# Moving attention, key selection and gate work of a five-branch decoder trunk against each other

## The chip, the cores and the metric

The kernel runs on one core of a Trainium2 chip. The metric is the device time in microseconds (us) of one execution, as the median of several runs. A profiled execution gives the trace. PE is the matrix engine (TensorE), DVE the vector engine, ACT the scalar engine, POOL the GpSimd engine, and SP the engine whose queue issues the weight transfers.

## The reference

Two layers (DEPTH = 2) over 512 tokens of width 1024. Each layer normalises the residual stream, projects it once with `w_in` (1024 x 12388), and feeds five branches:

```python
xn = rms_norm(h, norm_g[l])
(a_q, a_k, a_v, i_q, i_k, i_w, b_cq, b_ckv, b_kr, c_q, c_k, c_v,
 d_u, d_v, e_q, gates, merge) = jnp.split(xn @ w_in[l], offsets, axis=-1)
branches = (dsa_branch(...),     # A: 8 heads, one shared key/value head, best 128 keys per query
            mla_branch(...),     # B: 8 heads from low-rank latents, causal
            diff_branch(...),    # C: 4 heads, each the difference of two softmaxes, causal
            sgu_branch(...),     # D: chunked causal gating
            memory_branch(...))  # E: 4 heads over 256 memory tokens
mixed = sum(sigmoid(merge[n]) * ((o * silu(gates[n])) @ w_branch[l, n]) for n, o in enumerate(branches))
h = h + mixed @ w_out[l]
```

In A an indexer scores all earlier keys for each query (4 small heads, relu, weighted sum). The best min(256, 512 // 4) = 128 keys of each query are kept, and the softmax runs over those. In C two 64-row score matrices are made per head; the second softmax is multiplied by a lambda and subtracted from the first. A final RMS norm closes the trunk. Everything is float32.

## The kernel before, in words

**Precision and dense work.** Every float32 operand is split into a high and a low part (ACT copies the high part, DVE subtracts it to get the low part), and every product is three matmuls: high x high, high x low, low x high. These are lines 453 to 455, the helper `three`. Weights arrive through SP's queue as 512 KB pieces (`raw`), are split on the fly into `wh` (ACT, line 368) and `wl` (DVE, line 371), and the order of the pieces is the order of the units below. Up to four pieces are in flight and one or two are split ahead.

**Attention chains.** A, B and C share one chain per step, where a step is one head and one block of 128 queries (four blocks per head, so 32 steps for A, 32 for B, 16 for C; a step of C has two score matrices). PE makes scores into PSUM (`pS`); DVE adds the mask and takes the row maximum (`softmax_head`, line 543) and scales it (`nm`, line 546); ACT takes the exponential with the row sum (line 548); DVE takes the reciprocal (553); ACT normalises (554); PE transposes (`pT`, line 563); ACT and DVE split the result (185, 186); PE multiplies with the values (`po`, 573 or, in C, 1135). In C the normalisation is lines 1124 to 1128 on DVE, and row norms with a power on POOL follow (244). The chain is software-pipelined in `attend`: scores of step k, normalisation of step k-1, transposes of step k-2.

**Key selection for A.** `indexer` makes the four indexer heads and keys, then for each of the query blocks 1, 2, 3 a score tile of 256, 384 or 512 columns, and then 16 rounds of the DVE instructions MAX8 (line 1005: the eight largest of a row) and MATCH_REPLACE8 (line 1006: strike them out). Block 0 needs no selection. A's softmax uses the result as its mask, and A's first step is the one of block 3.

**What sets the order.** The string `ORDER` is the list of dense units of a layer, written by hand. `gX0 gX1` are the gates of branch X, `mX0` to `mX3` its merge and branch projection; `qr q0 q1 k0 k1 v0 v1` are B's latent projections; `a` A's queries; `ws dv z du` D's parts; `f0 f1 fv` C's queries with keys, and values; `mem` the next layer's memory rows. `+x` starts a chain, `-x` forces all that is left of it, `!x` forces a small postponed job. A planner (`Pace`) lets each chain advance between dense matmuls: every dense triple of matmuls lets planner time go by (660 ns for three 512-column ones, `tick`), and each part of a chain yields the planner time after which its next part may come. In attention that is `PACE`, 900 ns per part, for all branches. By the code a gate unit takes 10.6 us of planner time, a merge unit 15.9 us, and a unit of 512 output columns (`a dv du fv f0 f1`) 21.1 us.

This order is the priority of a list scheduler that then places the instructions on the engines, takes an instruction early if an older one can't go yet, and allocates buffers. On the chip each engine runs its instructions in the order so fixed.

**Buffers.** Most working tiles are blocks of 128 x 512 float32 from one pool of `NB` = 35 (2 KB per partition each). Four tiles `p` hold softmax rows. Three PSUM banks (tag `a`) serve scores, transposes and small jobs; four (tag `m`) serve the dense units; one (`o`) the products with the values. POOL's queue issues the loads of the memory rows, of D's small weights and of the residual rows (`h`).

Of the kernel before, what the change touches and what calls it, by code (L numbers as in the profile page):

```python
# [8 lines left out]
F32 = mybir.dt.float32  # L9
# [18 lines left out]
C_DU, C_DV, C_EQ, C_GATE, C_MERGE = 3172, 3684, 4196, 4708, 7268  # L28


ORDER = ("-mem gE0 !ckvt !lat qr q0 !qr0 gE1 k0 v0 +mla0 mE0 q1 k1 mE1 -mla0 !qr1 v1 +mla1 mE2 mE3 a -mla1 +idx "
         "gB0 gB1 mB0 mB1 mB2 mB3 !aq +dsa ws fv dv f0 z du -dsa !df0 +df0 f1 -df0 !oD !df1 "
         "gD0 gD1 +df1 mD0 mD1 -df1 mD2 mD3 gA0 gA1 mA0 mA1 mA3 mA2 gC0 gC1 mem mC0 mC1 mC3 mC2")
NW = 5
NB = 35
NC4 = 6
NTR = 8
NP = 4
NRAW = 4
PACE = 900.0  # L40
LAG_ROPE = 5000.0
LAG_QROPE = 10125.0
LAG_RSTD = 4000.0
# [89 lines left out]
def trunk(tc, d, out, taps=None):  # L133
    nc = tc.nc
# [439 lines left out]
                         start=(kb == 0 and n == 0), stop=(kb == 3 and n == len(ts) - 1))  # L574


    def attend(steps, scores, norm, trans, pv, pv_rows=None):

        hist = []
        due, last_due = None, None  # L580
        n = len(steps)
        for k in range(n + 4):
            cur = None
            if k < n:
                cur = scores(*steps[k][:2])
            if 0 < k <= n:
                norm(hist[k - 1], *steps[k - 1][:2])
            if cur is not None:
                hist.append(cur())
            yield PACE  # L590
            if last_due is not None:
                pv(last_due)
                last_due = None
                yield PACE
            if due is not None:
                u, i, last = due
                due = None
                if pv_rows is not None:
                    pv_rows(u, i)
                    if last:  # L600
                        last_due = u
                        yield LAG_FLIP
                    yield PACE
                elif last:
                    pv(u)
                    yield PACE
            if 2 <= k < n + 2:
                u, i, last = due = steps[k - 2]
                trans(hist[k - 2], u, i)
                hist[k - 2] = None  # L610
                yield PACE
        if last_due is not None:
            yield LAG_FLIP
            pv(last_due)
# [31 lines left out]
    def layer(l, mm):  # L646
        w = d["w_in"][l]
        S = {}
# [37 lines left out]
        def mem_attention():  # L686
            sc = 128 ** -0.5

            def scores(h, j):
                ps = psa("pS")  # L690
                kh, kl = (z[h // 2][:, (h % 2) * 256:(h % 2) * 256 + 256] for z in (S["kTh"], S["kTl"]))
                for jj in range(2):
                    q = slice((2 * j + jj) * 128, (2 * j + jj) * 128 + 128)
                    three(ps[:, jj * 256:(jj + 1) * 256], S["eh"][h][:, q], S["el"][h][:, q], kh, kl, True, True)

                def rest():
                    p = pp.tile([128, 512], F32, tag="p", name="p")
                    m, nm, s = small(2, "m"), small(2, "nm"), small(2, "s")
                    V.tensor_reduce(out=m, in_=ps.rearrange("p (j c) -> p j c", j=2), axis=AX.X, op=ALU.max)
                    V.tensor_scalar(nm, m, -sc, None, op0=ALU.mult)  # L700
                    for jj in range(2):
                        c = slice(jj * 256, (jj + 1) * 256)
                        A.activation(p[:, c], ps[:, c], AF.Exp, bias=nm[:, jj:jj + 1], scale=sc,
                                     accum_out=s[:, jj:jj + 1])
                    return p, s
                return rest

            def norm(ps_, h, j):
                p, s = ps_
                r = small(2, "r")  # L710
                V.reciprocal(r, s)
                for jj in range(2):
                    c = slice(jj * 256, (jj + 1) * 256)
                    V.tensor_scalar(p[:, c], p[:, c], r[:, jj:jj + 1], None, op0=ALU.mult)

            def trans(ps_, h, j):
                p = ps_[0]
                ps = psa("pT")
                for kb in range(2):
                    for jj in range(2):  # L720
                        T.transpose(ps[:, kb * 256 + jj * 128:kb * 256 + jj * 128 + 128],
                                    p[:, jj * 256 + kb * 128:jj * 256 + kb * 128 + 128], ident)
                src = ps.rearrange("p (k c) -> p k c", k=2)
                dst = [z[:, :1024].rearrange("p (k c) -> p k c", k=2)[:, :, j * 256:(j + 1) * 256] for z in pf]
                split(dst[0], dst[1], src)

            def pv(h):
                o = pso()
                c = slice(h * 128, h * 128 + 128)
                for kb in range(2):  # L730
                    three(o, S["mvh"][kb][:, c], S["mvl"][kb][:, c], pf[0][:, kb * 512:(kb + 1) * 512],
                          pf[1][:, kb * 512:(kb + 1) * 512], kb == 0, kb == 1)
                oT["E"][h] = blk(F32, "oE")
                A.activation(oT["E"][h], o, AF.Copy)

            yield 1500.0
            yield from attend([(h, j, j == 1) for h in range(4) for j in range(2)], scores, norm, trans, pv)
            tap(f"oE{l}", oT["E"][0])

        def go_mem():  # L740
# [189 lines left out]
        def mla_attention(hf):  # L930
            sc = 96 ** -0.5

            def scores(h, i):
                L = 128 * (i + 1)
                N = max(256, L)
                rows = slice(0, 96) if h % 2 == 0 else slice(0, 128)
                q = slice(i * 128, i * 128 + 128)
                ps = psa("pS")
                three(ps[:, :N], S["qh"][h][rows, q], S["ql"][h][rows, q], S["kh"][h][rows, :N],
                      S["kl"][h][rows, :N], True, True)  # L940
                return lambda: softmax_head(ps, L, cm[:, 512 - 128 * i:640], sc)

            def pv(h):
                o = pso()
                v = lambda kb: S["V"][kb][h // 4][:, h % 4, :, :].rearrange("p z c -> p (z c)")
                pv_causal(o, lambda kb: [(v(kb), 0), (v(kb), 1)])
                if h % 2 == 0:
                    oT["B"][h // 2] = blk(F32, "oB")
                r = slice(64 * (h % 2), 64 * (h % 2) + 64)
                add_halves(oT["B"][h // 2][r], o)  # L950

            yield 1500.0
            yield from attend(causal_steps(range(4 * hf, 4 * hf + 4)), scores,
                              lambda ps_, h, i: normalise(*ps_, 128 * (i + 1)),
                              lambda ps_, h, i: transposes(ps_[0], i), pv)
            if hf == 1:
                tap(f"oB{l}", oT["B"][0])
# [15 lines left out]
        def indexer():  # L973
# [10 lines left out]
            S["mb"] = [None] * 4  # L984
            for i in (1, 2, 3):
                L = 128 * (i + 1)
                sc = blk(F32, "score")
                S["mb"][i] = sc
                for hh in range(4):
                    ps = psa("pI")  # L990
                    q = S["iqs"][hh][:, i * 128:(i + 1) * 128]
# [5 lines left out]
                                           in1=cm[:, 512 - 128 * i:640] if hh == 0 else sc[:, :L],  # L997
                                           op0=ALU.mult, op1=ALU.add)
                    yield 900.0
                if i == 3:  # L1000
                    S["iqs"] = S["ki"] = None
                tap(f"score{l}_{i}", sc[:, :L])
                for _ in range(16):
                    m8 = small(8, "m8")
                    V.max(out=m8, in_=sc[:, :L])
                    V.match_replace(out=sc[:, :L], in_to_replace=m8, in_values=sc[:, :L], imm_value=GONE)
                    yield 700.0 + 2.0 * L
                V.tensor_scalar(sc[:, :L], sc[:, :L], -2e38, NEG, op0=ALU.is_gt, op1=ALU.mult)

        S["qs"] = [None] * 8  # L1010
# [28 lines left out]
        def dsa_attention():  # L1039
# [13 lines left out]
            def pv(h):  # L1053
# [3 lines left out]
                if h % 2 == 0:  # L1057
# [2 lines left out]
                add_halves(oT["A"][h // 2][r], o)  # L1060

            yield 500.0
            yield from attend(causal_steps(range(8)), scores,
                              lambda ps_, h, i: normalise(*ps_, 128 * (i + 1)),
                              lambda ps_, h, i: transposes(ps_[0], i), pv)
            tap(f"oA{l}", oT["A"][0])
# [36 lines left out]
        def diff_attention(hf):  # L1103
# [3 lines left out]
            def scores(e, i):  # L1107
                L = 128 * (i + 1)
                N = max(256, L)
                q = slice(i * 128, i * 128 + 128)  # L1110
                pss = []
                for s in range(2):
                    r = slice(64 * s, 64 * s + 64)
                    ps = psa("pS")
                    three(ps[:, :N], X["q"][e][0][r, q], X["q"][e][1][r, q], X["k"][e][0][r, :N],
                          X["k"][e][1][r, :N], True, True)
                    pss.append(ps)
                return lambda: [softmax_head(ps, L, cm[:, 512 - 128 * i:640], sc) for ps in pss]

            def norm(ps_, e, i):  # L1120
# [26 lines left out]
            def flip(e):  # L1147
                p = psa("pN")
                for i in range(4):
# [3 lines left out]

            X["o"] = {}
            yield 2500.0
            yield from attend(causal_steps(range(2)), scores, norm,
                              lambda ps_, e, i: transposes(ps_[0][0], i), flip, pv_rows)


# [339 lines left out]
```

## Time and profile before

| | |
|---|---|
| median of 3 runs | 1887.15 us (1886.16 to 1887.18) |
| profiled execution | 1887.75 us, of which its span is 1885.7 us |
| PE busy | 1802.5 us, 96% of the span |
| DVE busy | 1187.3 us, 63% |
| ACT busy | 947.3 us, 50% |
| POOL busy | 66.1 us, 4% |
| mean granted PE clock | 0.981 |

The span runs from the first to the last recorded instruction; 2.05 us of the profiled execution lie around it. Matmuls overlap in the pipeline, so the busy time of PE is a union and its idle time is what no matmul covers; the duration of one matmul is longer than the distance between two starts. The granted clock is listed beside each stretch of time: below 1.00 the array ran part of that stretch at a lower clock. The two layers are alike: what stands at time t of the first layer recurs some 932 us later.

### The profile page before, as it was taken

To read this page: it belongs to the slowest core of one execution; us is meant where nothing else is said; L and a number is where in the kernel's file an instruction comes from. 1 tells how busy PE (TensorE), PEld (TensorE's weight loads), DVE (VectorE), ACT (ScalarE), POOL (GpSimd) and SP (SyncE) were. 2 spreads that over 40 slices of the span, in tenths; PEclk is the share of its full clock that TensorE was granted. 3 is DMA by queue.
4 is the path that set the end of the run, shared out by engine and by line. 5 is a ranking of instruction groups with operands and counts; after the bars stand their busy time and mean duration, and the time that the engine had idled before them with its cause. 6 is when DMAs were issued, how large, how long until landed. Compare 5 with 4: busy or idle time off the path is not lost.

```text
span 1885.7 us, 24863 instructions
## 1 busy us (share of the span) xinstructions
PE 1802.5 (96%) x8793; PEld 1489.3 (79%) x8793; DVE 1187.3 (63%) x3009; ACT 947.3 (50%) x2127; POOL 66.1 (4%) x133
## 2 busy tenths in 40 slices
PE   7999999998899999999999999999898999999998
PEld 6878888886777778888887888888776776788887
DVE  7548756996656664445465577579967467544544
ACT  7457765426554553234355567653275545432333
POOL 1000000000000010000000000010000000000000
PEclk9999999999989999999999999999998999999999
DMA  6223222331212223333352332133311111233331
GB/s 230 73 73 87 62 79 84 95 90 45 68 34 57 68 73 106 101 116 97 117 174 56 73 98 68 56 101 101 90 44 47 56 56 57 74 94 101 118 127 69
DMA packets 151589, 161.02 MB, mean 85 GB/s; under 512 B 26293, under 2 KB 130793, under 8 KB 151465
## 3 DMA queue, kind: packets, MB, share of 16 engines
q1 hardware_dynamic: 148520, 149.21, 26.9%
q0 software_dynamic: 2944, 10.23, 1.6%
q8 instruction: 69, 1.13, 0.3%
q14 instruction: 56, 0.45, 0.1%
HBM read 155.22 MB, written 4.19 MB: 85 GB/s over the span
## 4 chain that ended last, share of the span: by engine, by line
PE 87%; DVE 7%; ACT 5%; issue 1%; DMA 0%; POOL 0%; POOLq 0%; SPq 0%; DVEq 0%; ACTq 0%
PE pm L453 25%; PE pm L454 25%; PE pm L455 25%; PE po L573 2%; PE pT L563 1%; PE pS L453 1%; DVE ptl L186 1%; DVE wl L371 1%; ACT p L548 1%; PE pS L454 1%; PE pS L455 1%; PE po L1135 1%; ACT p L554 1%; ACT pth L185 1%; PE pa L1020 1%
## 5 line engine op out<-in xcount | busy, mean ns | idle before, releaser
L371 DVE TENSOR_TENSOR wl<-raw,wh 128x512 fp32r<-128x512 f32 x556 | 376.2, 682 | 362.2 <-ACT wh L368 350.9
L368 ACT ACTIVATE wh<-raw 128x512 fp32r<-128x512 f32 x556 | 346.0, 625 | 512.5 <-PE pm L454 334.1
L453 PE MATMUL pm<-xh,wh 128*128 128x512 f32 x1040 | 410.3, 395 | 4.4 <-ACT nat L1013 1.7
L454 PE MATMUL pm<-xl,wh 128*128 128x512 f32 x1040 | 408.8, 393 | 0.0
L455 PE MATMUL pm<-xh,wl 128*128 128x512 f32 x1040 | 408.0, 393 | 0.0
L453 PEld LDWEIGHTS pm<-xh,wh 128*128 128x128 f32 x1040 | 196.4, 189 | 46.3 <-ACT nat L1013 2.2
L455 PEld LDWEIGHTS pm<-xh,wl 128*128 128x128 f32 x1040 | 196.2, 189 | 41.1 <-issue 0.7
L454 PEld LDWEIGHTS pm<-xl,wh 128*128 128x128 f32 x1040 | 196.4, 189 | 39.6 <-issue 0.6
L453 PE MATMUL pm<-wh,xh 128*128 128x512 f32 x512 | 202.1, 399 | 1.2 <-DVE acc L1304 1.2
L455 PE MATMUL pm<-wh,xl 128*128 128x512 f32 x512 | 202.5, 397 | 0.0
L454 PE MATMUL pm<-wl,xh 128*128 128x512 f32 x512 | 201.1, 393 | 0.0
L548 ACT ACTIVATE p<-p,nm 128x512 f32<-128x512 f32 (+1 forms) x192 | 107.3, 559 | 71.3 <-DVE nm L546 68.2
L453 PE MATMUL pm<-yh,wh 128*128 128x512 f32 x320 | 125.8, 393 | 0.0
L454 PE MATMUL pm<-yl,wh 128*128 128x512 f32 x320 | 125.6, 392 | 0.0
L455 PE MATMUL pm<-yh,wl 128*128 128x512 f32 x320 | 125.2, 391 | 0.0
L453 PEld LDWEIGHTS pm<-wh,xh 128*128 128x128 f32 x512 | 96.1, 188 | 22.3 <-issue 2.0
L455 PEld LDWEIGHTS pm<-wh,xl 128*128 128x128 f32 x512 | 96.2, 188 | 20.7 <-issue 0.5
L454 PEld LDWEIGHTS pm<-wl,xh 128*128 128x128 f32 x512 | 96.3, 188 | 18.2
L563 PE MATMUL pT<-ident,p 128*128 128x128 f32 x400 | 76.7, 294 | 34.2 <-ACT p L554 28.3
L186 DVE TENSOR_TENSOR ptl<-pT,pth 128x512 fp32r<-128x512 f32 (+3 forms) x176 | 88.6, 504 | 32.5 <-ACT pth L185 32.0
L185 ACT ACTIVATE pth<-pT 128x512 fp32r<-128x512 f32 (+3 forms) x176 | 78.7, 449 | 56.5 <-PE pT L563 40.9
L543 DVE CUSTOM_DVE_ANT_0 p<-pS,cm 128x128 f32<-128x128 f32 (+3 forms) x144 | 66.5, 462 | 47.0 <-PE pS L455 36.8
(337 smaller groups left out, 2940.1 us busy)
## 6 DMA issues: line engine op xcount, KB each, us to landing
raw<-w_in SPq DMA_DIRECT2D x176, 512.0 KB, 3.6
raw<-w_branch SPq DMA_DIRECT2D x40, 512.0 KB, 3.5
raw<-w_in SPq DMA_DIRECT2D x36, 256.0 KB, 3.0
raw<-mem_w_kv SPq DMA_DIRECT2D x16, 512.0 KB, 5.2
raw<-w_out SPq DMA_DIRECT2D x16, 512.0 KB, 3.8
raw<-mla_w_uq SPq DMA_DIRECT2D x18, 128.0 KB, 3.4
xrow<-x SPq DMA_DIRECT2D x4, 512.0 KB, 7.4
raw<-mla_w_ukv SPq DMA_DIRECT2D x16, 128.0 KB, 2.5
```

The source lines that it names most:

```text
L185: A.activation(hi, src, AF.Copy)
L186: V.tensor_tensor(out=lo, in0=src, in1=f32(hi), op=ALU.subtract)
L368: A.activation(hv, raw, AF.Copy)
L371: V.tensor_tensor(out=lv, in0=raw, in1=f32(hv), op=ALU.subtract)
L453: T.matmul(o, ah, bh, start=st, stop=False)
L454: T.matmul(o, ah, bl, start=False, stop=False)
L455: T.matmul(o, al, bh, start=False, stop=sp)
L543: V.tensor_tensor_reduce(out=p[:, :L], in0=ps[:, :L], in1=mask, op0=ALU.add, op1=ALU.max, scale=1.0, scalar=GONE, accum_out=m)
L548: A.activation(p[:, :L], p[:, :L], AF.Exp, bias=nm, scale=scale, accum_out=s)
L554: A.activation(p[:, :L], p[:, :L], AF.Copy, scale=r)
L563: T.transpose(ps[:, kb * 128:(kb + 1) * 128], p[:, kb * 128:(kb + 1) * 128], ident)
L573: T.matmul(o[:, q0:], v, pf[part][:, kb * 384 + q0:kb * 384 + 512], start=(kb == 0 and n == 0), stop=(kb == 3 and n == len(ts) - 1))
```

## The change

Six things are changed.

1. **Early selection.** `+idx` moves from behind `-mla1` to right behind `!lat`, ahead of B's projections. All three score tiles are now made first, which lets the indexer's query and key tiles go; then the 48 rounds follow, each pair of instructions yielding 1500 + 3.0 L instead of 700 + 2.0 L ns of planner time (L = 256, 384, 512).
2. **Longer steps.** `attend` takes the branch's name, and `PACE` is 900 ns for E, 1200 for B, 1900 for A, 1600 for C.
3. **The order.** `mE2` and `gB0` now lie inside B's two halves. A's attention starts ahead of `mB0` to `mB3` and runs beside them too. `fv` goes behind `du`. C's first half is no longer forced right behind `f1`: it runs beside `f1 gD0 gD1 mD0 mD1`, and its second half beside `mD2 mD3 gA0 gA1 mA0 mA1`.
4. **Paired scores in C.** The two 64-row score matrices of a step are written alternately, product by product, into two PSUM banks, instead of one after the other. The products are the same.
5. **41 blocks** instead of 35.
6. The scratch memory for the descriptors of POOL's transfers is set to 4096 bytes, which makes room for the blocks.

```diff
-ORDER = ("-mem gE0 !ckvt !lat qr q0 !qr0 gE1 k0 v0 +mla0 mE0 q1 k1 mE1 -mla0 !qr1 v1 +mla1 mE2 mE3 a -mla1 +idx "
-         "gB0 gB1 mB0 mB1 mB2 mB3 !aq +dsa ws fv dv f0 z du -dsa !df0 +df0 f1 -df0 !oD !df1 "
-         "gD0 gD1 +df1 mD0 mD1 -df1 mD2 mD3 gA0 gA1 mA0 mA1 mA3 mA2 gC0 gC1 mem mC0 mC1 mC3 mC2")
+ORDER = ("-mem gE0 !ckvt !lat +idx qr q0 !qr0 gE1 k0 v0 +mla0 mE0 q1 k1 mE1 mE2 -mla0 !qr1 v1 +mla1 mE3 a gB0 -mla1 gB1 "
+         "!aq +dsa mB0 mB1 mB2 mB3 ws dv f0 z du fv -dsa !df0 +df0 f1 !oD gD0 gD1 mD0 mD1 -df0 !df1 "
+         "+df1 mD2 mD3 gA0 gA1 mA0 mA1 -df1 mA3 mA2 gC0 gC1 mem mC0 mC1 mC3 mC2")
-NB = 35
+NB = 41
-PACE = 900.0
+PACE = {"E": 900.0, "B": 1200.0, "A": 1900.0, "C": 1600.0}
...
-    def attend(steps, scores, norm, trans, pv, pv_rows=None):
+    def attend(branch, steps, scores, norm, trans, pv, pv_rows=None):
+        gap = PACE[branch]
...
-            yield PACE
+            yield gap
...
             for i in (1, 2, 3):
                 L = 128 * (i + 1)
-                sc = blk(F32, "score")
-                S["mb"][i] = sc
+                sc = S["mb"][i] = blk(F32, "score")
...
-                if i == 3:
-                    S["iqs"] = S["ki"] = None
+            S["iqs"] = S["ki"] = None
+            for i in (1, 2, 3):
+                L = 128 * (i + 1)
+                sc = S["mb"][i]
                 for _ in range(16):
                     m8 = small(8, "m8")
                     V.max(out=m8, in_=sc[:, :L])
                     V.match_replace(out=sc[:, :L], in_to_replace=m8, in_values=sc[:, :L], imm_value=GONE)
-                    yield 700.0 + 2.0 * L
+                    yield 1500.0 + 3.0 * L
...
-                pss = []
-                for s in range(2):
-                    r = slice(64 * s, 64 * s + 64)
-                    ps = psa("pS")
-                    three(ps[:, :N], X["q"][e][0][r, q], X["q"][e][1][r, q], X["k"][e][0][r, :N],
-                          X["k"][e][1][r, :N], True, True)
-                    pss.append(ps)
+                pss = [psa("pS") for _ in range(2)]
+                rows = [slice(64 * s, 64 * s + 64) for s in range(2)]
+                for n, (a, b) in enumerate(((0, 0), (0, 1), (1, 0))):
+                    for ps, r in zip(pss, rows):
+                        T.matmul(ps[:, :N], X["q"][e][a][r, q], X["k"][e][b][r, :N], start=n == 0, stop=n == 2)
...
-    nc = bacc.Bacc("TRN2", target_bir_lowering=False, num_devices=1)
+    nc = bacc.Bacc("TRN2", target_bir_lowering=False, num_devices=1, dynamic_dma_scratch_size=4096)
```

More of the change, by code (lines that the diff above doesn't have):

```diff
@@ L593, in attend @@
                 last_due = None
-                yield PACE
+                yield gap
             if due is not None:
@@ L602, in attend @@
                         yield LAG_FLIP
-                    yield PACE
+                    yield gap
                 elif last:
                     pv(u)
-                    yield PACE
+                    yield gap
             if 2 <= k < n + 2:
@@ L610, in attend @@
                 hist[k - 2] = None
-                yield PACE
+                yield gap
         if last_due is not None:
@@ L736, in mem_attention @@
             yield 1500.0
-            yield from attend([(h, j, j == 1) for h in range(4) for j in range(2)], scores, norm, trans, pv)
+            yield from attend("E", [(h, j, j == 1) for h in range(4) for j in range(2)], scores, norm, trans, pv)
             tap(f"oE{l}", oT["E"][0])
@@ L952, in mla_attention @@
             yield 1500.0
-            yield from attend(causal_steps(range(4 * hf, 4 * hf + 4)), scores,
+            yield from attend("B", causal_steps(range(4 * hf, 4 * hf + 4)), scores,
                               lambda ps_, h, i: normalise(*ps_, 128 * (i + 1)),
@@ L1062, in dsa_attention @@
             yield 500.0
-            yield from attend(causal_steps(range(8)), scores,
+            yield from attend("A", causal_steps(range(8)), scores,
                               lambda ps_, h, i: normalise(*ps_, 128 * (i + 1)),
@@ L1155, in diff_attention @@
             yield 2500.0
-            yield from attend(causal_steps(range(2)), scores, norm,
+            yield from attend("C", causal_steps(range(2)), scores, norm,
                               lambda ps_, e, i: transposes(ps_[0][0], i), flip, pv_rows)
```

## The prediction

> **What bounds the kernel now.** The page's slices and its chain come first.
>
> ```profile
> PE   7999999998899999999999999999898999999998
> DVE  7548756996656664445465577579967467544544
> ```
> ```profile
> PE 87%; DVE 7%; ACT 5%; issue 1%; DMA 0%; POOL 0%; POOLq 0%; SPq 0%; DVEq 0%; ACTq 0%
> ```
>
> PE holds the end, and its low slices lie in the attention of each layer. So only two things can shorten the run: PE's idle or slow-clocked time, and PE's own work. The next view cuts the run by stage; its columns are engine busy times with instruction counts, the granted PE clock and DMA.
>
> ```profile
> core 0: us, PE busy (x) PEld busy (x) DVE busy (x) ACT busy (x) POOL busy (x), PEclk, DMA share, GB/s
> 147.00:172.00 25.00, 25.00 (x141) 21.74 (x140) 22.86 (x45) 17.25 (x32) 0.00 (x0) 1.00 0.34 90
> 172.00:302.00 130.00, 125.34 (x641) 105.15 (x640) 81.82 (x238) 89.06 (x204) 0.00 (x0) 1.00 0.21 64
> 302.00:347.00 45.00, 45.00 (x223) 37.73 (x222) 35.58 (x73) 25.96 (x48) 5.64 (x6) 1.00 0.41 118
> 347.00:410.00 63.00, 63.00 (x280) 52.24 (x279) 61.61 (x148) 20.86 (x36) 0.00 (x0) 1.00 0.34 100
> 410.00:548.00 138.00, 119.40 (x558) 95.92 (x557) 95.21 (x290) 82.72 (x204) 2.68 (x4) 0.90 0.16 46
> 565.00:708.00 143.00, 136.69 (x649) 105.53 (x648) 91.37 (x313) 70.09 (x190) 11.82 (x20) 0.96 0.22 67
> 708.00:855.00 147.00, 147.00 (x650) 121.71 (x649) 68.22 (x105) 49.31 (x84) 1.08 (x2) 1.00 0.36 108
> 1342.00:1480.00 138.00, 118.69 (x557) 95.52 (x555) 94.10 (x289) 81.82 (x203) 2.67 (x4) 0.90 0.16 46
> 1497.00:1638.00 141.00, 133.56 (x643) 101.95 (x642) 91.07 (x313) 69.48 (x188) 9.66 (x16) 0.99 0.21 61
> ```
>
> In the first layer B's attention is 172 to 302, selection 302 to 434, A's attention 410 to 548 and C's 565 to 708; the last two rows are A and C of the second layer. The dense stretch 708 to 855 has no idle time and gives the price of a 512-column matmul, 147.00 / 650 = 0.226 us, and of DVE beside gates and merges, 68.22 / 147 = 0.46 us per us. A loses 138 - 119.40 = 18.6 us of idle and, at clock 0.90, up to 0.10 x 138 = 13.8 us of speed. B has as many steps of nearly the same chain and loses 130 - 125.34 = 4.7 us at full clock. C loses 6.3 us idle and 0.04 x 143 = 5.7 us of clock, in the second layer 7.4 and 1.4. What ends A's waits, and the worst of them:
>
> ```profile
> PE pT L563 <- ACT p L554: 12.6, 5, 6.1
> ```
> ```profile
> 429.56 0.39 PE L455 MATMUL pm<-wh,xl 128*128 128x512 f32 x1
> 436.00 0.69 PE L563 MATMUL pT<-ident,p 128*128 128x128 f32 x2 [6.05 <-ACT p L554]
> ```
> ```profile
> 432.80 0.43 DVE L1008 TENSOR_SCALAR score<-score 128x512 f32<-128x512 f32 x1
> 433.26 0.69 DVE L543 CUSTOM_DVE_ANT_0 p<-pS,score 128x512 f32<-128x512 f32 x1
> ```
>
> Of the stretch's waits, 12.6 us end with the normalised row that the transposes need. In the worst one selection ends on DVE at 433.2, A's first softmax starts at once, and PE stands at the transposes although dense matmuls follow in its order: the chain is too near behind its own inputs.
>
> **A's attention, longer steps.** By the code A yields 76 times: 68 us of planner time at 900 ns, 144 at 1900. Ahead of its forced end lie four units and `z`, 87 us; with `mB0` to `mB3` it is 151. (A triple counts 0.66 us in the planner and 3 x 0.226 = 0.68 on PE.) Now the chain has about 4.3 us of dense work per step instead of 2.0, more than B has today. No instruction of A is added. If A then loses what B loses, 4.7 us, the gain per layer is between 18.6 - 4.7 = 13.9 (idle alone) and 18.6 + 13.8 - 4.7 = 27.7 us; the second layer has 14.6 to 28.4. I take **26 a layer, -52**, near the upper end, because PE was mostly busy while slow: its rows give 119.40 us busy at a mean clock of 0.90. The bounds for two layers are 0 (the waits only move) and -66 (all of it). [...]
>
> **C's attention, no forced end.** A half of C yields 30 times and waits twice for a flip, 31 us with its lead, beside `f1`, 21 us; the rest is forced out without dense work. At 1600 it is 52 us beside 74, and 84 for the second half. Of 12.0 and 8.8 us lost I leave 4 each: 8.0 + 4.8, **-13**; bounds 0 and -21.
>
> **C's paired scores.** The trace already holds pairs: the scheduler put two score products of different row halves side by side wherever both banks were free.
>
> ```profile
> 581.46 0.39 PE L454 MATMUL pm<-wl,xh 128*128 128x512 f32 x1
> 581.77 0.38 PE L453 MATMUL pS<-kh,qh 64*128 64x256 f32 x1
> ...
> 582.32 0.50 PE L455 MATMUL pm<-wh,xl 128*128 128x512 f32 x1
> 582.66 0.40 PE L453 MATMUL pm<-wh,xh 128*128 128x512 f32 x1
> ```
> ```profile
> 592.67 0.28 PE L1135 MATMUL po<-dv,ptl 128*128 128x256 f32 x1
> 592.88 0.51 PE L453 MATMUL pS<-kh,qh 64*128 64x512 f32 x2
> ...
> 593.78 0.50 PE L453 MATMUL pm<-wh,xh 128*128 128x512 f32 x1
> 594.12 0.40 PE L454 MATMUL pm<-wl,xh 128*128 128x512 f32 x1
> ```
> ```profile
> 1589.86 0.39 PE L455 MATMUL pm<-yh,wl 128*128 128x512 f32 x1
> 1590.18 0.39 PE L453 MATMUL pS<-kh,qh 64*128 64x256 f32 x2
> ...
> 1590.73 0.39 PE L1135 MATMUL po<-dv,pth 128*128 128x256 f32 x1
> 1590.96 0.28 PE L1135 MATMUL po<-dv,ptl 128*128 128x256 f32 x1
> ```
>
> One unpaired half of 256 columns costs 582.66 - 581.46 less two dense matmuls, 1.20 - 0.45 = 0.75 us. Both halves paired cost 1590.96 - 1589.86 less one dense matmul and one 256-column product (half a dense one, 0.11), 0.76 us: the second half is free. At 512 columns both halves cost 594.12 - 592.67 - 0.11 - 0.226 = 1.11 us. So a new pair saves 0.75 to 1.11 us. Of the 32 score steps 8 are paired already (the first at 592.88, the last at 1590.18) and 4 partly: 20 new pairs save 15 us, with the parts and the wide ones up to 19. I take **-13**; bounds 0 and -19. [...] I expect most pairs to form because at 1600 ns the banks are read before the next step.
>
> **Early selection beside B.**
>
> ```profile
> L1005 DVE MAX8 m<-score 128x8 f32<-128x256 f32 (+2 forms) x96 | 53.2, 558 | 1.4
> L1006 DVE MATCH_REPLACE8 score<-m,score 128x256 f32<-128x256 f32 (+2 forms) x96 | 52.2, 544 | 0.1
> ```
> ```profile
> 410.00:434.00 24.00, 17.97 (x38) 1.00 0.30 87
> ```
>
> The rounds take (53.2 + 52.2) / 2 = 53 us of DVE per layer. Until now they ran beside dense units, and DVE was full (61.61 of 63 us) while PE lost nothing; they ended late all the same, at 433, and held A (the last row is the score tile's DVE time behind 410). From the start of B's projections to A, DVE does 22.9 + 81.8 + 35.6 + 61.6 + 18.0 = 220 us. `mB0` to `mB3` leave this stretch: 65 us of PE, and at 0.46 some 30 of DVE. What is left is 190 us of DVE in 263 - 65 = 198 of PE, 96%, and B's chain, today at 81.8 / 130 = 63%, runs in it. Queued behind a round on DVE are B's maxima, reciprocals and low parts, for which ACT and PE wait, and the `wl` parts. No row shows this mix. From below: B's 4.7 us a layer vanish, as its steps grow from 900 to 1200 ns, -9. From above: B stalls as A does, +27.7 a layer, +55. I take **+12**, nearer to the lower end, because a full DVE cost PE nothing in 347 to 410, and the rounds, at 1500 + 3 L, leave gaps. The planner gives selection 141 us in 139, so one round is forced at A's start; if it is late again, A waits, but `mB0` to `mB3` now lie behind A's first scores as dense work.
>
> **At nothing.** Moved gates and merges keep their instructions, and PE had no gap beside them. Their weights follow them in SP's queue, four pieces ahead. More blocks only allow earlier allocation. For POOL's scratch:
>
> ```profile
> h<-hscr POOLq DMA_DIRECT2D x4, 512.0 KB, 4.7
> ```
> ```profile
> 1831.47 1.05 POOL L1382 DMA_DIRECT2D h<-hscr  x2 [83.16 <-PE pm L455]
> ```
> ```profile
> 1851.84 0.69 DVE L1393 SCALAR_TENSOR_TENSOR h<-pm,h 128x512 f32<-128x512 f32 x1
> ```
>
> Even if its transfers had to go one behind the other, four such loads would take 19 us, and 20 us lie between the issue of the last ones and their first use. Without that cover they cost up to 10 us over both layers; there is no reason for a gain.
>
> **Sum.** -52 - 13 - 13 + 12 = -66 us. The profiled execution took 1887.75 us (span 1885.7 and 2.05 around it), which gives 1821.75; the median of the runs is 0.6 lower, so **1821 us**.
>
> **Rivals.** (1) *Selection spoils B*: half of the upper bound, +27.7 instead of +12, with PE standing at B's transposes: 1837; at the full bound 1864. For it: 96% of DVE. Against: DVE at 98% without loss in 347 to 410. (2) *A's waits move*: the chain is bound by its own latency, or starts late, and A saves only the lower bound, 28 instead of 52: 1845. For it: ACT and DVE are busy only 60 and 69% in A and PE waits all the same. Against: B's rows. (3) *Slower: DVE becomes the bound from B's projections to A.* With chains beside it DVE reaches only the share it has in A, 95.2 / 138 = 69%; then 190 us of DVE take 275 instead of 198 us, +77 a layer against a gain of 39 (26 + 6.5 + 6.5): 1887 + 2 x 38 = 1963. It decides below a DVE share of 190 / (198 + 39) = 80%. [...] Against: 302 to 347 ran at 79% without idle PE. (4) *It does nothing*: one loss replaces the other, 1887.
>
> **Chances and range.** Forecast 0.66 (own range 1800 to 1838), (1) 0.14, (2) 0.12, (3) 0.05, (4) 0.03. The low end, 1793, is -66 - 21 of the bounds for A and C with 13 for pairs and +5 for B. The high end, 1865, holds (2) and (1) at its full bound. A difference under 0.2% can't be told from none. Faster 0.92, same 0.03, slower 0.05.
>
> **What would show it.** Right: A's stretch at clock 1.00 with under 8 us idle; no single wait above 3 us; rows of `pS` in C with x2 in most steps; PE near 98% busy. Wrong: PE waits of B's `pT` or `pS` on DVE adding up to more than 10 us a layer; selection ending far behind A's first scores with PE idle; waits on ACT's row as before.

## The result and the profile after

| | before | changed |
|---|---|---|
| median | 1887.16 us (1886.16 to 1887.64, 4 runs) | 1830.05 us (1825.94 to 1834.69, 4 runs) |
| profiled execution (its span) | 1887.75 us (1885.7) | 1825.94 us (1823.9) |
| mean granted PE clock | 0.981 | 0.996 |

The ratio is 0.9699, with a 95% interval from 0.9669 to 0.9729: 57 us less, where 66 were forecast. The four runs of the changed kernel fall on two levels, 1826 (twice) and 1834 (twice), which widens the interval; the last section comes back to this. The profile is of a run on the lower level, so sums from the profiles come to 62 us instead of 57.

From the page of the changed kernel, busy time by engine, PE's slices and the chain's shares:

```profile
PE 1774.7 (97%) x8793; PEld 1470.2 (81%) x8793; DVE 1179.6 (65%) x3009; ACT 944.0 (52%) x2127; POOL 67.7 (4%) x133
...
PE   7999999999999999999999999999999999999998
...
PEclk9999999999999999999999999999999999999999
...
PE 93%; DVE 4%; ACT 1%; issue 1%; DMA 0%; SPq 0%; POOL 0%; POOLq 0%; DVEq 0%; ACTq 0%
```

The low slices of A and C are gone, and PE's share of the chain that ended last rose from 87 to 93%. The same stages as windows of the changed kernel (columns as in the prediction's table). In the first layer 107 to 351 is the lead-up, from the end of E's attention to A's first scores, with the selection and B in it; 351 to 539 is A, 547 to 696 is C. The last three rows are the same three stages of the second layer.

```profile
107.00:351.00 244.00, 231.05 (x1163) 191.78 (x1161) 197.17 (x525) 148.10 (x321) 8.41 (x16) 1.00 0.28 79
147.00:351.00 204.00, 191.05 (x967) 158.09 (x965) 177.86 (x479) 128.79 (x275) 5.20 (x6) 1.00 0.27 77
351.00:539.00 188.00, 186.63 (x918) 155.78 (x919) 117.24 (x312) 108.99 (x248) 2.96 (x4) 0.99 0.25 73
547.00:696.00 149.00, 149.00 (x710) 116.15 (x707) 98.50 (x310) 69.00 (x182) 7.43 (x12) 1.00 0.25 75
1008.00:1252.00 244.00, 232.98 (x1164) 193.10 (x1162) 198.58 (x524) 148.46 (x321) 8.44 (x16) 0.99 0.28 79
1252.00:1441.00 189.00, 187.18 (x921) 156.16 (x922) 117.74 (x313) 109.50 (x248) 2.97 (x4) 0.99 0.25 73
1448.00:1628.00 180.00, 180.00 (x862) 142.04 (x862) 117.35 (x355) 84.93 (x219) 10.50 (x16) 1.00 0.26 77
```

The lead-up of the kernel before, in the same view:

```profile
107.00:408.00 301.00, 296.34 (x1464) 248.78 (x1463) 218.78 (x543) 172.04 (x363) 8.84 (x16) 1.00 0.30 84
```

A is idle for 1.4 us where it lost 18.6, C for nothing. The lead-up got worse: 13.0 us idle against 4.7, though it holds fewer units. PE's waits over the whole of the changed kernel say the same. The columns are who waited for whom, the total in us, how often, and the longest:

```profile
PE pa L225 <- DMA vec<-mla_kv_norm_g: 6.7, 1, 6.7
PE pm L453 <- DVE acc L1304: 5.0, 4, 1.9
PE pm L453 <- DVE sg L1278: 4.4, 4, 1.5
PE po L453 <- ACT pth L185: 3.5, 4, 1.5
PE pI L992 <- DVE iqs L965: 3.3, 2, 1.6
```

The largest entry of the kernel before, the wait of the transposes for ACT's normalised row, has gone from the list:

```profile
PE pT L563 <- ACT p L554: 28.3, 12, 6.1
```

What has come are single waits under 2 us: for gates (`sg`) and for the indexer's queries (`iqs`), which the list before does not have, and for merges (`acc`), 5.0 us instead of 2.5. The wait at the top of the list is in both kernels (6.8 us before).

**One yardstick for all kernels.** For each matmul I take the distance from its start to the next start in the trace, less the usual distance of its width in the traces of both kernels (227 ns for 512 columns, 174 for 384, 119 for 256, 109 for 128). The usual distances add up to 1727.4 us in both kernels, so the whole difference lies in what is left over, called *lost time* below. It holds waits, slow clock and the cost of the 64-row scores together.

| lost time, us (layer 1 / layer 2) | before | changed |
|---|---|---|
| lead-up (indexer, selection, B) | 8.5 / 8.5 | 19.4 / 19.6 |
| A's attention | 34.4 / 34.5 | 5.6 / 5.5 |
| C's attention | 21.6 / 20.8 | 8.1 / 8.3 |
| all else, both layers | 16 | 16 |

A gave 58 us, C gave 26, the lead-up took 22 back. The sum is 62, and the two profiled executions differ by 1887.75 - 1825.94 = 61.8.

### The profile page after: what moved, and what is told of

It reads as the page before. It is cut to its first block, busy times and chain, and to the rows that moved or that the text cites. A ratio compares the mean times of both kernels' runs of the same rounds, so it can differ in the third digit from the quotient of the medians.

```text
span 1823.9 us, 24819 instructions
## 1 busy us (share of the span) xinstructions
PE 1774.7 (97%) x8793; PEld 1470.2 (81%) x8793; DVE 1179.6 (65%) x3009; ACT 944.0 (52%) x2127; POOL 67.7 (4%) x133
## 4 chain that ended last, share of the span: by engine, by line
PE 93%; DVE 4%; ACT 1%; issue 1%; DMA 0%; SPq 0%; POOL 0%; POOLq 0%; DVEq 0%; ACTq 0%
PE pm L453 27%; PE pm L454 26%; PE pm L455 26%; PE po L573 2%; PE pT L563 2%; PE pS L1117 2%; PE po L1135 1%; DVE wl L371 1%; PE pa L526 1%; PE pS L455 1%; PE pS L454 1%; PE pS L453 1%; DVE score L1008 1%; PE pS L1050 1%; PE pa L1022 1%
## 5 line engine op out<-in xcount | busy, mean ns | idle before, releaser
L453 PEld LDWEIGHTS pm<-wh,xh 128*128 128x128 f32 x512 | 96.1, 188 | 20.2 <-issue 2.2
L554 ACT ACTIVATE p<-p,r 128x512 f32<-128x512 f32 (+3 forms) x128 | 71.6, 559 | 24.7 <-DVE r L553 24.4
```

Source lines behind the costliest of these rows:

```text
L453: T.matmul(o, ah, bh, start=st, stop=False)
L554: A.activation(p[:, :L], p[:, :L], AF.Copy, scale=r)
```

## The experiments

Theory L says that the longer steps carry A's gain. Theory D says that the rounds of the selection, now on DVE beside B, cost the lead-up its new loss. Theory P1 says that pairs of scores do not form because two banks are not free together. The rivals stand with each run. All changes are made to the changed kernel unless "before" is named.

### Is it the rounds? (D)

The selection makes 3 of its 48 rounds per layer; the other 45 are left out, so A's mask is not the reference's here.

```diff
-                for _ in range(16):
+                for _ in range(1):
```

> The changed kernel (1830 us) with 45 of the 48 selection rounds of each layer left out, so A's mask is not the reference's; all else in place. Theory D (the rounds on DVE beside B's chain are what the early selection costs): DVE loses some 49 us a layer in the stretch ahead of A, its share there falls from about 90% to about 65%, PE's idle time in that stretch falls to B's old 5 us a layer, and the time falls by about 30 to 1800 us. Rival (the early tiles, the moved units or the shortage of blocks delay B, not DVE): 1825 to 1830 us, the waits in B's stretch stay.

Measured: 1814.13 us, ratio 0.9616 (0.9595 to 0.9636). The lead-up's lost time fell from 19.4 / 19.6 to 13.9 / 14.7, A's from 5.6 / 5.5 to 4.0 / 4.0. Its first lead-up as a window:

```profile
107.00:351.00 244.00, 234.48 (x1183) 195.13 (x1182) 160.63 (x405) 151.34 (x329) 8.49 (x16) 1.00 0.29 79
```

With 160.63 instead of 197.17 us of DVE in the same 244 us, PE still stands idle for 9.5 us. So D is half right: the rounds cost 16 us over both layers by the medians and 13 by the profiles, of which 10 are in the lead-up (half of its 22) and 3 in A. The other half stays without them. D's 1800 us did not come.

### Early selection without the rest

Before, with `+idx` moved up, all score tiles first, the longer yields of the rounds, 41 blocks and the smaller scratch; A, B and C keep their places and 900 ns.

```diff
-ORDER = ("-mem gE0 !ckvt !lat qr q0 !qr0 gE1 k0 v0 +mla0 mE0 q1 k1 mE1 -mla0 !qr1 v1 +mla1 mE2 mE3 a -mla1 +idx "
+ORDER = ("-mem gE0 !ckvt !lat +idx qr q0 !qr0 gE1 k0 v0 +mla0 mE0 q1 k1 mE1 -mla0 !qr1 v1 +mla1 mE2 mE3 a -mla1 "
...
-NB = 35
+NB = 41
...
-                    yield 700.0 + 2.0 * L
+                    yield 1500.0 + 3.0 * L
```

> The kernel before (1887 us) with the early selection alone: selection begins ahead of B's projections at the slower rounds, with 41 blocks and the smaller scratch; order of all dense units, steps of 900 ns and C as before. Theory D: B's stretch loses about 15 us a layer more on a fuller DVE, and A saves only its wait for the last rounds, 6 us a layer: about 1887 + 31 - 12 = 1905 us, slower than before. Rival (A lost its time to rounds and softmax sharing DVE, so freeing DVE is what A gained): A saves its 33 us a layer here too and the time is 1887 + 31 - 66 = 1852 us.

Measured: 1888.81 us beside 1888.73 for the kernel before, ratio 1.0001 (0.999 to 1.0012). Neither number came. Its windows of the first lead-up and of A, and the worst of A's waits:

```profile
108.00:418.00 310.00, 298.90 (x1460) 247.64 (x1459) 231.58 (x581) 172.59 (x363) 8.45 (x16) 1.00 0.29 82
418.00:546.00 128.00, 114.24 (x562) 93.87 (x561) 79.58 (x254) 82.43 (x204) 2.68 (x4) 0.95 0.18 52
```
```profile
PE pT L563 <- ACT p L554: 7.3, 4, 4.3
```

A does gain: its clock goes from 0.90 to 0.95, the wait for ACT's row from 12.6 to 7.3 us, and its lost time from 34.4 / 34.5 to 23.4 / 23.9. The lead-up gives as much back: 18.5 / 20.2 against 8.5 / 8.5. Moved by itself, the selection takes its cost from A to B. No run has the changed kernel with the selection back in its old place, so what the early selection is worth beside the other changes is not shown.

### Short steps everywhere (L)

```diff
-PACE = {"E": 900.0, "B": 1200.0, "A": 1900.0, "C": 1600.0}
+PACE = {"E": 900.0, "B": 900.0, "A": 900.0, "C": 900.0}
```

> The changed kernel with 900 ns for all branches; order, early selection, pairs and blocks stay. Theory L (the longer steps give the chain the time it needs): A runs its steps with 2 us of dense work each as before and loses about 30 us a layer again, C some 5, B gains nothing: 1890 to 1900 us. Rival (it is enough that more dense work lies in the order behind the chain, since the scheduler takes it whenever the chain is late): 1825 to 1840 us.

Measured: 1859.26 us, ratio 0.9853 (0.9836 to 0.987), between the two forecasts, neither of which came. The window of A's attention and its first wait:

```profile
367.00:485.00 118.00, 110.19 (x533) 89.96 (x532) 75.15 (x227) 76.65 (x180) 1.14 (x2) 0.96 0.21 59
```
```profile
PE pT L563 <- ACT p L554: 3.7, 2, 2.8
```

The waits for ACT's row are back, but shorter. A loses 16.3 / 17.4 us, C 15.1 / 18.4, the lead-up 15.9 / 14.6. So the longer steps of A, B and C together hold 29 of the 57 us by the medians. By lost time they give 23 us in A and 17 in C and take 9 in the lead-up, 31 of the 34 between the two profiles. L, which lets them carry all of A's gain, is right for less than half of it. Followed from run to run, A's 29 us per layer come in three parts: 34.4 to 23.4 by the earlier selection (the run above), to 16.3 by the rest of the change at 900 ns, above all the new order in which A runs beside the merges of B, and to 5.6 by the longer steps. Another sequence of runs could share them out otherwise.

### C's rearrangement alone

Before, with C's part of the order and 1600 ns for C; the scores not paired.

```diff
-         "gB0 gB1 mB0 mB1 mB2 mB3 !aq +dsa ws fv dv f0 z du -dsa !df0 +df0 f1 -df0 !oD !df1 "
-         "gD0 gD1 +df1 mD0 mD1 -df1 mD2 mD3 gA0 gA1 mA0 mA1 mA3 mA2 gC0 gC1 mem mC0 mC1 mC3 mC2")
+         "gB0 gB1 mB0 mB1 mB2 mB3 !aq +dsa ws fv dv f0 z du -dsa !df0 +df0 f1 !oD gD0 gD1 mD0 mD1 -df0 !df1 "
+         "+df1 mD2 mD3 gA0 gA1 mA0 mA1 -df1 mA3 mA2 gC0 gC1 mem mC0 mC1 mC3 mC2")
...
+        gap = 1600.0 if branch == "C" else PACE
```

> The kernel before (1887 us) with C's rearrangement alone: both halves of C run beside the gates and merges at 1600 ns and are no longer forced behind f1; scores unpaired, everything else as before. Theory: C's waits and slow clock go, 11 us a layer: about 1865 us. Rival (C gained because A ended on time and fv moved): 1880 to 1887 us.

Measured: 1865.62 us, ratio 0.9883 (0.9868 to 0.9898), 23 us less than before, as expected. C's first window of this kernel:

```profile
565.00:687.00 122.00, 121.52 (x588) 94.81 (x588) 75.37 (x234) 56.47 (x142) 5.33 (x8) 1.00 0.27 77
```

Idle 0.5 us, clock 1.00: 23 of the 26 us that C gave are there without a change to the scores.

### The scores of C: does the new loop pair them?

The first run takes the old loop, `three` for one half and then for the other. The second ties the six matmuls of the new loop so that the scheduler keeps them in their written order.

```diff
-                for n, (a, b) in enumerate(((0, 0), (0, 1), (1, 0))):
-                    for ps, r in zip(pss, rows):
-                        T.matmul(ps[:, :N], X["q"][e][a][r, q], X["k"][e][b][r, :N], start=n == 0, stop=n == 2)
...
+                for s in range(2):
...
+                    three(ps[:, :N], X["q"][e][0][r, q], X["q"][e][1][r, q], X["k"][e][0][r, :N],
+                          X["k"][e][1][r, :N], True, True)
```
```diff
...
+                        with contextlib.nullcontext() if prev is None else tc.issue_after(prev):
+                            prev = T.matmul(ps[:, :N], X["q"][e][a][r, q], X["k"][e][b][r, :N], start=n == 0,
+                                            stop=n == 2).ins
```

> The changed kernel (1830 us) with C's two score matrices of a step again one after the other. The traces show 30 score matmuls right beside their partner of the other row half after the change and 26 before, so the new loop by itself formed few pairs. Theory P1 (pairs depend on two free PSUM banks, not on the order in the loop): 0 to 4 us slower, within 1826 to 1839. Rival (the pairs carry C's gain): 13 to 19 us slower, about 1846 us.

> The changed kernel with the six score matmuls of a step of C tied in their order, so that the second product of the first half can't be issued before the first product of the second half. Nothing is waited for but the order of issue; the scheduler puts dense matmuls in between while a bank is missing. In the fixed order 136 of 160 possible neighbours alternate, against 44 in the changed kernel. Theory P1: about 20 more steps save 0.4 to 0.75 us each, 8 to 15 us: 1815 to 1822 us. Rival (the first half then holds its bank longer and C's chain falls behind): C's stretch shows new waits, 1830 us or more.

Measured: unpaired 1833.8 us (1826.41 to 1834.23), ratio 0.9697 (0.9673 to 0.9721), the same as the changed kernel; tied 1825.64 us, ratio 0.967 (0.965 to 0.969). The old loop gives the same runs of 64-row matmuls on PE as the new one: 42 groups of three (one half alone), 8 of six (a pair), 2 of nine (a pair and a half). The next rows, of the changed kernel, show how such groups come about (`x2` marks two that start together):

```profile
546.62 0.49 PE L1117 MATMUL pS<-kh,qh 64*128 64x512 f32 x2
...
546.96 0.39 PE L1117 MATMUL pS<-kl,qh 64*128 64x512 f32 x2
...
547.19 0.40 PE L1117 MATMUL pS<-kh,ql 64*128 64x512 f32 x2
...
547.42 0.34 PE L1117 MATMUL pS<-kh,qh 64*128 64x384 f32 x1
...
548.05 0.50 PE L453 MATMUL pm<-wh,xh 128*128 128x512 f32 x1
548.05 0.68 DVE L543 CUSTOM_DVE_ANT_0 p<-pS,cm 128x512 f32<-128x512 f32 x1
```
```profile
553.87 0.56 DVE L543 CUSTOM_DVE_ANT_0 p<-pS,cm 128x384 f32<-128x384 f32 x1 [0.45 <-PE pS L1117]
...
555.58 0.38 PE L1117 MATMUL pS<-kh,qh 64*128 64x256 f32 x1
...
556.40 0.41 DVE L543 CUSTOM_DVE_ANT_0 p<-pS,cm 128x256 f32<-128x256 f32 x1
...
557.02 0.38 PE L1117 MATMUL pS<-kh,qh 64*128 64x256 f32 x1
```

The first step takes two of the three banks, paired. The scheduler then fills the third with the first half of the *next* step at 547.42, before anything has been read. In the next steps each half goes out alone behind a read by DVE (555.58 behind the read at 553.87, 557.02 behind the one at 556.40). That fits P1, but the trace does not show that a bank was missing: when the half at 555.58 started, DVE had read all earlier scores (the last by 554.43), and so it is in 9 of the 11 steps of the first layer that went as two lone halves. PE's order was fixed beforehand by the scheduler, and no run shows when the scheduler took a bank for free. Tying the six matmuls makes more of them neighbours: the 64-row scores, with entering and leaving that shape, cost 41.7 us in place of 45.5 by the distances of starts. But in 22 of the 32 steps the first matmul still goes alone, with dense ones between it and the other five. P1's 1815 to 1822 us did not come, and the gain in time stays within what the two levels blur.

### The rest of the lead-up

Two runs go to its other half: B at its former 900 ns, and the planner's pause ahead of A's query work (behind the split of A's keys) at 3200 instead of 800 ns, so that this work comes after the indexer's. A third starts A two units later, with A's steps and the rounds stretched.

```diff
-PACE = {"E": 900.0, "B": 1200.0, "A": 1900.0, "C": 1600.0}
+PACE = {"E": 900.0, "B": 900.0, "A": 1900.0, "C": 1600.0}
```
```diff
-            yield 800.0
+            yield 3200.0
```
```diff
-         "!aq +dsa mB0 mB1 mB2 mB3 ws dv f0 z du fv -dsa !df0 +df0 f1 !oD gD0 gD1 mD0 mD1 -df0 !df1 "
+         "mB0 mB1 !aq +dsa mB2 mB3 ws dv f0 z du fv -dsa !df0 +df0 f1 !oD gD0 gD1 mD0 mD1 -df0 !df1 "
...
-PACE = {"E": 900.0, "B": 1200.0, "A": 1900.0, "C": 1600.0}
+PACE = {"E": 900.0, "B": 1200.0, "A": 1550.0, "C": 1600.0}
...
-                    yield 1500.0 + 3.0 * L
+                    yield 1875.0 + 3.75 * L
```

> The changed kernel (1830 us; two levels, 1826 and 1834) with B's steps back at 900 ns and all else changed. Between the end of E's attention and A's first scores the changed kernel loses 19.4 and 19.6 us of PE time against its matmul prices, with all steps at 900 ns 15.9 and 14.6. Theory B (longer steps of B stretch its chain over more of the selection and cost 3 to 5 us a layer): 1822 to 1826 us. Rival (that difference came from A and C starting elsewhere, B's step is neutral): 1828 to 1832 us.

> The changed kernel with 3200 instead of 800 ns of planner time between the indexer's last transposes and its first score product, so that some 30 matmuls stand between them in PE's order instead of none. Theory S (part of the early selection's price is not the rounds but the indexer's start: PE stands at the first pI products for 1.6 us a layer on the low part of iqs and some 2 us more behind it): 4 to 8 us less, 1822 to 1826 us. Rival (the wait is only moved to the next thing that DVE owes PE, since DVE is full there): 1828 to 1832 us.

> The changed kernel with A started behind mB0 and mB1 instead of ahead of them, its steps 1550 instead of 1900 ns so that they still fit, and the rounds spread 25% wider. Theory D: the stretch ahead of A has 33 us more of PE's work with some 15 of DVE, DVE's share falls, and half of the 15 us a layer that B lost comes back while A loses up to 3: 1815 to 1825 us. Rival (B's stretch is not short of DVE): 1830 us or, as A is tighter, some us more.

Measured: B at 900 1820.85 us, ratio 0.964 (0.9626 to 0.9654); the pause 1825.14, ratio 0.9668 (0.9655 to 0.9682); the later start 1828.85, ratio 0.9695 (0.9672 to 0.9717), which is no change; Theory D's 1815 to 1825 did not come. The changed kernel's PE in the order of time, around the two places where B's halves are forced out (262 to 268 and 348 to 354); the first row is the merge just ahead of the first place:

```profile
256.87 0.50 PE L453 MATMUL pm<-yh,wh 128*128 128x512 f32 x1 [1.95 <-DVE acc L1304]
...
265.58 0.50 PE L573 MATMUL po<-ptl,mlaV 128*128 128x512 f32 x1 [1.41 <-DVE ptl L186]
...
268.21 0.38 PE L453 MATMUL pm<-wh,ckvh 128*128 128x256 f32 x1 [0.95 <-ACT mth L1293]
...
349.61 0.51 PE L573 MATMUL po<-pth,mlaV 128*128 128x512 f32 x1 [1.58 <-ACT pth L185]
```

With B at 900 ns none of these four is left. That kernel's waits in the same stretch, 107 to 351, have for `po` no more than the first line below; the second is its window, whose idle time is 8.0 us instead of 13.0:

```profile
PE po L573 <- ACT pth L185: 0.4, 1, 0.4
...
107.00:351.00 244.00, 236.05 (x1158) 196.69 (x1158) 190.27 (x513) 144.03 (x315) 8.80 (x16) 0.97 0.27 74
```

So B's longer step was a loss by itself. At 1200 ns a rest of B is still open at both of its forced ends, and PE stands between its scores, transposes and products with no dense matmul in between, just as C did before. By the medians this loss is 9 us, and 5 against the changed kernel's lower level; the two profiles differ by 3.6 only, because this run met a clock of 0.97 in that stretch, against 1.00.

The pause takes the wait for `iqs` off the list, and the idle time of the two lead-ups falls by 6 us. But the clock is 0.99 in both in this profile, against 1.00 and 0.99, the lost time hardly moves (19.0 / 18.9 instead of 19.4 / 19.6), and the 5 us between the medians are within the two levels. So the indexer's start is not shown to be a cause of the lead-up's loss.

### 35 blocks

```diff
-NB = 41
+NB = 35
```

(and the former scratch memory for POOL's descriptors).

> The changed kernel with 35 blocks and the former scratch. Theory: blocks only allow earlier allocation, and early selection holds 5 more of them over B: a few us, 1830 to 1840. Rival (B's stretch waits for blocks even with 41): more than 15 us slower, with PE waits on evacuations into B's tiles in that stretch.

Measured: 1832.93 us, ratio 0.9706 (0.9682 to 0.9729), 3 us above the changed kernel's median and within its two levels. A's lost time rose to 10.2 / 10.1, the lead-up's fell to 16.3 / 16.6.

### Better than both

The first run joins B at 900, the longer pause and the tied scores. The second, whose edit follows, leaves the scores untied and gives C steps of 2200 ns instead.

```diff
-PACE = {"E": 900.0, "B": 1200.0, "A": 1900.0, "C": 1600.0}
+PACE = {"E": 900.0, "B": 900.0, "A": 1900.0, "C": 2200.0}
...
-            yield 800.0
+            yield 3200.0
```

> The changed kernel with B's steps at 900 ns, the indexer's 3200 ns and C's six score products tied in their order, together. If the three savings add: 4 from the tied order (1825.6 measured against 1830), 5 from B, 5 from the indexer: about 1815 us. If DVE's share ahead of A is the limit whatever is moved there, only the tied order's part remains: 1825 us.

> The changed kernel with B at 900 ns, the pause before A's later query work at 3200 ns, and C's steps at 2200 instead of 1600 ns. In the order of instructions 92 of the 160 neighbouring 64-row score matmuls now lie on different row halves, against 44 in the changed kernel. Theory P1 (pairs fail for want of two free banks; a longer step of C leaves two free): the 64-row scores cost 38 to 40 us instead of 45.5, and the time is 1812 to 1817, against 1817 for the same kernel with tied scores. Rival (pairs are worth little where C is late at its forced end): 1819 or more, with idle time of PE at C's forced ends.

Measured: 1817.06 us, ratio 0.9626 (0.9612 to 0.9639), and **1812.54 us, ratio 0.9609 (0.9596 to 0.9622)**. The second beats the kernel before by 74 us and the changed one by 17. Its 64-row scores cost 39.0 us instead of 45.5, inside P1's 38 to 40. The groups of 256-column scores by line, first of the changed kernel, then of the one with 2200 ns (busy time, mean ns of one):

```profile
L1117 PE MATMUL pS<-kh,qh 64*128 64x256 f32 x32 | 12.3, 383 | 0.0
L1117 PE MATMUL pS<-kl,qh 64*128 64x256 f32 x32 | 8.9, 278 | 0.0
```
```profile
L1117 PE MATMUL pS<-kh,qh 64*128 64x256 f32 x32 | 10.0, 382 | 0.0
L1117 PE MATMUL pS<-kl,qh 64*128 64x256 f32 x32 | 7.2, 277 | 0.0
```

One matmul takes as long as before (382 ns), but busy time is a union, and it falls because more of them run together: 16 groups of six instead of 8, 26 single halves instead of 42. P1's forecast came, and more time between two steps of C pairs the halves where the loop did not. That the free banks are the reason stays argued: no run gave the scores a fourth bank.

## Why the prediction was right, and where its steps were not

The forecast was 1821 us with a range from 1793 to 1865; 1830.05 lies in it, and faster by more than 0.2% was given 0.92. That the sum came so near is in part luck: the paired scores came out 13 us and the early selection 10 us worse than forecast, C's rearrangement 10 us and A 6 us better.

- **What bounds the kernel: right.** PE's idle and slow-clocked time was all that moved; the usual distances add up to the same 1727.4 us.
- **A, -52: right, measured -58.** Each layer gave 29 us (26 forecast, 28 if A came down to what B loses). The step took idle *and* clock as one loss, and both went: 0.90 to 0.99, 18.6 us idle to 1.4. But the longer steps that I named as the cause hold only 11 of the 29; along the runs above the earlier selection holds 11 and the new order 7.
- **C, no forced end, -13: mechanism right, size wrong.** "Of 12.0 and 8.8 us lost I leave 4 each" is the failed term. Nothing was left (149.00 of 149 and 180.00 of 180 us busy at clock 1.00), and the rearrangement alone gave 23, a little over the bound of 21.
- **Paired scores, -13: failed.** "I expect most pairs to form because at 1600 ns the banks are read before the next step" is the step. The banks mostly were read before the next step (9 of the 11 unpaired steps of the first layer), and the pairs did not form all the same: 42 halves still went alone, and the new loop gave the same time as the old one. That the scheduler puts halves side by side "wherever both banks were free" is not borne out by these reads. The worth of a pair was right: with 2200 ns, 8 more pairs save 6.5 us, 0.8 us each (0.75 to 1.11 forecast).
- **Early selection, +12: too low, measured +22.** I reckoned with DVE's load alone, 96% of the stretch, and had it too high; the trace has 177.86 of 204 us, 87%. The rounds did cost half of the 22, about the +12 that I took. What I had not priced is B's own step of 1200 ns, which I counted only as a gain ("as its steps grow from 900 to 1200 ns, -9") and which costs up to 9 us by running B into its forced ends. This is not the whole account: with B at 900 ns the early selection alone already cost the lead-up 22 us, the rest of the change at 900 ns took 8 of them off, and the longer steps put 9 on. The last round ends where the planner's sum put it, at A's first scores (350.95). In the changed kernel's answer for the line of the rounds, the third and fourth number are the first and last start in us:

```profile
L1008 DVE MATCH_REPLACE8 score<-m,score x48: 400/542/686, 165.7 to 351.8; 128x256 f32<-128x256 f32 x16, 128x384 f32<-128x384 f32 x16, 128x512 f32<-128x512 f32 x16
```

- **At nothing.** Blocks and scratch: about 3 us in the median, not told apart from nothing by their runs.
- **The rivals.** *Selection spoils B* is in part what happened (its 1837 lies as near to 1830 as the forecast's 1821), but through waits under 2 us for gates, merges and forced ends, not through B's transposes. *A's waits move* and *it does nothing* fall with A's windows. *DVE becomes the bound* falls with DVE at 87% beside a PE that is 94% busy (191.05 of 204).
- **What would show it.** A idle under 8 us, no inner wait above 3 us and PE near 98% held (1.4, 1.9, 97%); `x2` in most of C's steps did not: 10 of 32. The 6.7 us at the start of the program, in both kernels, is left aside.

## What to carry to other kernels

Where a scheduler interleaves chains with dense work, size each chain's steps so that it ends just before its forced end. Too short, and PE stood at the chain (before, A idle for 18.6 of 138 us and C for 6.3 of 143); too long, and the forced rest ran bare (B at 1200 ns, the lead-up idle for 13.0 us against 8.0 at 900). Moving the selection out of A's way put its cost in the lead-up (A's lost time 34.4 to 23.4 us, the lead-up's 8.5 to 18.5); by itself it was worth nothing here (ratio 1.0001). Whether two half-height matmuls ran together was settled by the order that the scheduler fixed, not by the loop in which they are written (8 groups of six with either loop, 16 with steps of 2200 ns): count the pairs in the trace, and try more time between the steps.

## What the runs showed that was not expected

**The same waits, two clocks.** The two levels of the changed kernel, 1826 and 1834 us, differ in the granted clock: its mean is 0.996 in both runs of the lower level and 0.990 in both of the upper. The profile of the changed kernel is of the lower level. The kernel with the old score loop, which has the same two levels, was profiled at 1834.23 us, and at the end of E's attention, where its instructions are those of the changed kernel, both have the same waits. First the changed kernel's PE in time and the windows that follow:

```profile
97.93 0.50 PE L453 MATMUL po<-pth,mvh 128*128 128x512 f32 x1 [0.29 <-ACT pth L185]
...
102.12 0.49 PE L453 MATMUL po<-pth,mvh 128*128 128x512 f32 x1 [1.46 <-ACT pth L185]
```
```profile
99.00:103.20 4.20, 2.39 (x11) 1.57 (x11) 2.52 (x8) 2.94 (x14) 0.00 (x0) 1.00 0.21 57
103.20:107.20 4.00, 4.00 (x18) 3.25 (x18) 1.94 (x8) 1.20 (x7) 0.00 (x0) 1.00 0.00 0
```

Then the same of the run with the old loop:

```profile
98.77 0.50 PE L453 MATMUL po<-pth,mvh 128*128 128x512 f32 x1 [0.29 <-ACT pth L185]
...
102.96 0.50 PE L453 MATMUL po<-pth,mvh 128*128 128x512 f32 x1 [1.46 <-ACT pth L185]
```
```profile
100.00:104.00 4.00, 2.19 (x11) 1.42 (x10) 2.38 (x8) 2.90 (x14) 0.00 (x0) 1.00 0.20 56
104.00:108.00 4.00, 4.00 (x11) 3.15 (x11) 1.97 (x9) 1.24 (x7) 0.00 (x0) 0.57 0.00 0
```

After the same waits one run went on at full clock (1.00), the other at 0.57 in the mean of the next 4 us, 11 matmuls in place of 18. Where that run was slow throughout a window its clock was 0.50 (358 to 362 us), so I estimate (1 - 0.57) x 4 / (1 - 0.50) = 3.4 us of half speed. From 100 to 366 us the slower profile has four such places (windows at 0.50 to 0.84 within 104 to 108, 160 to 168, 259 to 266 and 354 to 366 us); the faster one has three from its start to PE's last matmul (at 0.69 to 0.89 within 350 to 358, 1076 to 1084 and 1251 to 1259 us). The longest wait ahead of the slow stretch shown here is 1.46 us, in 4 us of which PE was busy for 2.19; right ahead of the three of the faster profile the longest are 1.58, 0.92 and 1.58 us. What decides between the two clocks is open.

**A's waits were worth more than their length.** A's 29 us per layer stand against 17 us of idle time in the windows (18.6 to 1.4). By the clocks of the same windows (0.90 and 0.99) I estimate the rest: 0.10 x 138 us before and 0.01 x 188 us after differ by 12 us.
